# Hymba-style encoder block on one Trainium2 core: a12's quarter of the second half loaded in the raw ring, the x2 loads and pair sums spread over the stages, and the first last block in two passes

## The chip, the cores and the metric

The kernel runs on one core of one Trainium2 chip. The engines are called PE (matrix product), DVE (vector), ACT (scalar), POOL (GpSimd) and SP (which here issues the DMA transfers). The metric is the device time of one execution in microseconds (us); the figure for the kernel before is a median of three timed runs. A trace of one more execution, taken by the hardware profiler, shows each instruction.

## The reference

The block takes x of 2048 tokens by 1024 features and adds three residual terms: a mixer (short convolution and bidirectional gated linear attention), cross-attention into 256 memory rows, and an MLP. A final RMSNorm closes it. The change touches only the end of it:

```python
def sq_relu_mlp(x, mlp_norm, w_up, w_down):
    h = rms_norm(x, mlp_norm) @ w_up          # 1024 -> 4096
    return jnp.square(jax.nn.relu(h)) @ w_down  # 4096 -> 1024
...
        x = x + sq_relu_mlp(x, mlp_norm[l], w_up[l], w_down[l])
    return rms_norm(x, final_norm)
```

All is float32. The kernel keeps that accuracy by splitting each operand into a rounded high part and a low rest, and by forming three products: high by high, high by low, low by high.

## The kernel before, in words

Features lie on the 128 partitions and tokens on the free axis. A tile of a product is 128 features by 512 tokens and fills one PSUM bank; there are eight banks, four named `ps` and four named `pg`, which the code takes in turn. Tiles in SBUF come from rings of fixed depth: `a` (28 tiles of 128x1024, for operands and for the residual x2), `g` (8, for split weights), `st` (2 tiles of 128x2048), `raw` and `cv` (3 each, for what has just been loaded), `t` (7) and `gt` (8). A load into a ring waits until the last reader of that ring's oldest tile is done. SP issues the DMA transfers in one fixed order, so a load that waits for its tile holds up all loads behind it. Three helpers stand behind most rows of the profile: `split` (L117 the high part on ACT, L118 the low part on DVE), `add` (L928, on DVE unless POOL is named) and `mm3` (L145 to L147, three matmuls).

**Up projection.** It is done in two halves of the tokens (`hf` = 0, 1), each with the seven products of a Strassen-like scheme for every one of 16 weight steps f (L1013). `token_side` prepares the seven token operands: it loads four quarters of the normalised tokens (a11, a22, a21, a12) from the DRAM tile `x2d` by `quarter` (loads at L956, scaling in four operations at L960), then adds, subtracts and splits. a11, a21 and a12 lie in the `st` ring, a22 in `raw` and `cv`. As `st` has two tiles, which a11 and a21 hold, a12's loads wait until a11 has been read for the last time. The token side of the second half is made while the last steps of the first half run. `weight_side` loads each step's weights into `raw` and `cv` (L990), and forms and splits the seven weight operands. The results, squared after the ReLU, go out to the DRAM tile `zu` (L1019, L1023).

**Down projection.** 28 of the 32 row tiles of `w_down` are taken in four groups of 4, 4, 3 and 3 pairs (GROUPS). For each group, `half_steps` yields 14 steps: seven products for each of two token halves c, in the order 1, 2, then 5, 3, then 6, 4 and 7, each pair of lines for c = 0 and c = 1. `token_operands` reads `zu` back (L1125 into `raw` and `cv`, L1152 into `st`) and combines the pieces on POOL or DVE; `weight_operands` reads `w_down` (L1171) into `t` and `gt` and subtracts on POOL. Operands are prepared up to three steps ahead. Each step has four banks (d = 0 to 3) of 12 matmuls each (L1243, 9 in the groups of 3). Products 2 and 3 go on in the banks of 1 and 5. Each bank is then evicted by `add` into the residual `acc`, or into `sums`, the sum u that three quarters of the output share. `acc` holds x2, eight d by two c, in 16 tiles of the `a` ring, loaded by `load_acc` (L1218): d 0 to 3 ahead of the loop, d 4 to 7 at step 0. After the loop, 24 additions on DVE (128x512) put the shared sums into three quarters of `acc`: the pair sums, which the trace shows as `a<-a,a`.

**Last blocks.** The remaining four row tiles (REST) are added in five blocks of tokens by `column`: for each d of eight one bank with 12 matmuls over j = 0 to 3, eviction into `acc`, square on ACT, and the sum of the squares on POOL (DVE in the last block). `rest_u` loads and splits the four token operands of a block, `load_w` the four weight operands. `finish` turns the sum of squares of a block into the RMSNorm's factors and scales and stores the block's output (L1287) while the next block's matmuls run. For these blocks the order on PE and DVE is that in which the code is written.

Of the kernel before, what the change touches and what calls it, by code (L numbers as in the profile page):

```python
# [10 lines left out]
F32R = mybir.dt.float32r  # L11
# [6 lines left out]
P = 128  # L18
S = 2048
D = 1024  # L20
KT = D // P
TB = 512
# [8 lines left out]
def block_kernel(ctx, tc, x, mem, wm, wv, wlg, wlog, wout, wxk, wxv, wxqT, wxo, wup, wdn,  # L31
                 vecs, ones, consts, out):
    nc = tc.nc
# [7 lines left out]
    def A4(dt=F32, shape=(P, 1024)):  # L41
        return big.tile(list(shape), dt, tag="a", name="a4", bufs=NA)
# [7 lines left out]
    def RAW(shape=(P, 1024)):  # L50
        return big.tile(list(shape), F32, tag="raw", name="raw", bufs=3)

    def CV():
        return big.tile([P, 1028], F32, tag="cv", name="cv", bufs=3)
# [54 lines left out]
    zu = dram.tile([FF, S], F32, name="zu")  # L109
# [6 lines left out]
    def split(src, hi, lo):  # L116
        mark["act"] = nc.scalar.copy(hi, src)  # L117
        nc.vector.tensor_tensor(out=lo, in0=src, in1=hi.bitcast(F32), op=ALU.subtract)  # L118
# [10 lines left out]
    def load_w(ap, shape=(P, 1024), T=A4):  # L129
        r = RAW(shape)  # L130
        mark["dma"] = nc.sync.dma_start(r, ap)
        hi, lo = T(F32R, shape), T(F32R, shape)
        split(r, hi, lo)
        return hi, lo
# [8 lines left out]
    def mm3(ps, L, R, first, last):  # L143
        (lh, ll), (rh, rl) = L, R
        nc.tensor.matmul(ps, lh, rh, start=first, stop=False)  # L145
        nc.tensor.matmul(ps, lh, rl, start=False, stop=False)  # L146
        mark["pe"] = nc.tensor.matmul(ps, ll, rh, start=False, stop=last)  # L147
# [31 lines left out]
    def fold(tiles, SQ, eng):  # L179

        acc = None
        for t in tiles:
            sq = SQ()
            nc.scalar.activation(sq, t, AF.Square)
            if acc is None:
                acc = sq
            else:
                eng.tensor_tensor(out=acc, in0=acc, in1=sq, op=ALU.add)
        eng.tensor_tensor(out=acc[:, 0], in0=acc[:, 0], in1=acc[:, 1], op=ALU.add)
        return acc[:, 0]  # L190
# [574 lines left out]
    with tc.manual_schedule(engines={EngineType.PE}):  # L765
# [6 lines left out]
        sq = fold([mt[:, 2 * j:2 * j + 2] for mt in mts for j in range(2)], lambda: T2(F32, (P, 2, NMEM)), nc.vector)  # L772
# [118 lines left out]
    for b in range(4):  # L891
        bs = slice(b * TB, (b + 1) * TB)
        yb, nxt = nxt, []
        if b == 3:

            xts, pss = [], []
# [5 lines left out]
            for kt in range(KT):  # L902
                for d in range(KT):
                    ds = slice(d * P, (d + 1) * P)
# [5 lines left out]
        for dp in range(KT // 2):  # L910
            ld = y_load(b + 1, dp)
            xt = load_T(x, b, dp, CV()[:, :D].rearrange("p (j t) -> p j t", j=2))
            for j in range(2):
                d = 2 * dp + j
                ds = slice(d * P, (d + 1) * P)
                ps = PS()
# [10 lines left out]
    def add(out, a, b, op=ALU.add, eng=nc.vector):  # L927
        eng.tensor_tensor(out=out, in0=a, in1=b, op=op)  # L928
# [11 lines left out]
    def S2():  # L940
        t = ST(F32, (P, 2, 1024))
        return [t[:, i] for i in range(2)]

    def R2():
        return [RAW(), CV()[:, :D]]
# [5 lines left out]
    def quarter(hf, b, k, t):  # L951

        b0 = 2 * hf + b
        for i in range(2):
            r = (4 * k + 2 * i) * P
            nc.sync.dma_start(t[i].rearrange("p (j t) -> p j t", j=2),  # L956
                              x2d[r:r + 2 * P, b0 * TB:(b0 + 1) * TB].rearrange("(j p) t -> p j t", p=P))
        for j, v in enumerate(kts(t)):
            kt = 4 * k + j
            nc.vector.scalar_tensor_tensor(out=v, in0=v, scalar=g_mlp[:, kt:kt + 1], in1=rows[:, b],  # L960
                                           op0=ALU.mult, op1=ALU.mult)
        return t

    def token_side(hf):

        a11 = quarter(hf, 0, 0, S2())
        a22 = quarter(hf, 1, 1, R2())
        a21 = quarter(hf, 1, 0, S2())  # L970
        yield None
        yield 1, operand(a11)
        yield 4, operand(a22)
        s = a22
        both(s, a21, a22, ALU.add)
        yield 5, operand(s)
        both(s, s, a11, ALU.subtract)
        yield 6, operand(s)
        both(a21, a11, a21, ALU.subtract)
        a12 = quarter(hf, 0, 1, S2())  # L980
        yield 2, operand(a12)
        yield 7, operand(a21)
        both(a12, a12, s, ALU.subtract)
        yield 3, operand(a12)
# [131 lines left out]
    GROUPS = [(0, 16, 4), (4, 20, 4), (8, 24, 3), (11, 27, 3)]  # L1116
    REST = (14, 30, 15, 31)
# [96 lines left out]
    def load_acc(ds):  # L1214
        for d in ds:
            for c in range(2):
                acc[d][c] = A4()
                nc.sync.dma_start(acc[d][c], x2d[d * P:(d + 1) * P, c * 1024:(c + 1) * 1024])  # L1218

    halves = [slice(0, TB), slice(TB, 2 * TB)]  # L1220
    steps = half_steps()
    ahead = [next(steps)]
    acc = [[None, None] for _ in range(KT)]
    load_acc(range(4))
    sums = [A4(F32, (P, 2, TB)) for _ in range(4)]
    for i in range(14 * len(GROUPS)):
        while len(ahead) < 3:
            ahead.append(next(steps, None))
        first, p, c, w, x = ahead.pop(0)
        if i == 0:  # L1230
            load_acc(range(4, KT))
        n = len(x)

        chained = p in (2, 3)
        if not chained:
            banks = [(PG if d % 2 == 0 else PS)() for d in range(4)]
        for d in range(4):
            ds = slice(d * P, (d + 1) * P)
            ps = banks[d]
            for k in range(n):  # L1240
                wh, wl = w[k][0][:, ds], w[k][1][:, ds]
                for l, r in ((wh, x[k][0]), (wh, x[k][1]), (wl, x[k][0])):
                    nc.tensor.matmul(ps, l, r, start=not chained and k == 0 and l is wh and r is x[k][0],  # L1243
                                     stop=k == n - 1 and l is wl, skip_group_check=chained)
            o11, o21 = (acc[d][c][:, h] for h in halves)
            o12, o22 = (acc[d + 4][c][:, h] for h in halves)
            u = sums[d][:, c]
            if p == 1 and first:
                nc.scalar.copy(u, ps)
                continue  # L1250
            for o in {1: (u,), 2: (o11,), 6: (u,), 5: (o22,), 3: (o12,), 7: (o21, o22), 4: (o21,)}[p]:
                if p == 4:
                    add(o, o, ps, SUB)
                else:
                    add(o, ps, o)


    def rest_u(b):
        got = []
        for i in range(0, 4, 2):  # L1260
            t = (RAW() if i == 0 else CV()[:, :D]).rearrange("p (j t) -> p j t", j=2)
            for j in range(2):
                f = REST[i + j]
                nc.sync.dma_start(t[:, j], zu[f * P:(f + 1) * P, b * TB:(b + 1) * TB])
            hi, lo = (A4(F32R, (P, 2, TB)) for _ in range(2))
            split(t, hi, lo)
            got += [(hi[:, j], lo[:, j]) for j in range(2)]
        return got

    ur = [rest_u(0)]  # L1270
    wr = [load_w(wdn[f], T=G4) for f in REST]
    for d in range(4):
        for c in range(2):
            u = sums[d][:, c]
            for o in (acc[d][c][:, halves[1]], acc[d + 4][c][:, halves[0]], acc[d + 4][c][:, halves[1]]):
                add(o, o, u, eng=nc.vector)

    def final_sums(sq, n, PT):
        m = n // P
# [7 lines left out]
        nc.vector.scalar_tensor_tensor(out=a, in0=a, scalar=g_fin[:, d:d + 1], in1=r, op0=ALU.mult, op1=ALU.mult)  # L1287
        nc.sync.dma_start(out[d * P:(d + 1) * P, c * 1024 + cs.start:c * 1024 + cs.stop], a)

    def column(us, c, cs, squares, between):  # L1290

        qs = []
        n = cs.stop - cs.start
        o = cs.start % TB
        for d in range(KT):
            ds = slice(d * P, (d + 1) * P)
            ps = (PG if d % 2 == 0 else PS)()[:, :n]
            for j in range(4):
                mm3(ps, (wr[j][0][:, ds], wr[j][1][:, ds]), (us[j][0][:, o:o + n], us[j][1][:, o:o + n]), j == 0, j == 3)
            a = acc[d][c][:, cs]  # L1300
            add(a, ps, a)
            qs.append(GT()[:, :n])
            nc.scalar.activation(qs[-1], a, AF.Square)
            if d > 1:
                add(qs[0], qs[0], qs[d - 1], eng=squares)
            if between is not None:
                next(between, None)
        add(qs[0], qs[0], qs[-1], eng=squares)
        return qs[0]
# [12 lines left out]
    blocks = [(0, cs) for cs in halves] + [(1, halves[0]), (1, slice(TB, TB + TH)), (1, slice(TB + TH, 2 * TB))]  # L1322
    todo = None
    with tc.manual_schedule(engines={EngineType.PE, EngineType.DVE}):
        for n, (c, cs) in enumerate(blocks):
            if n + 1 < 4:
                ur.append(rest_u(n + 1))
            sq = column(ur[min(n, 3)], c, cs, nc.vector if n == len(blocks) - 1 else nc.gpsimd, todo)
            for _ in todo or ():
                pass  # L1330
            todo = finish(c, cs, sq)
        for _ in todo:
            pass
# [60 lines left out]
```

## Time and profile before

| | us |
|---|---|
| median of three timed runs | 2694.26 (2693.18 to 2695.48) |
| profiled execution | 2702.45 |
| its span | 2700.7 |
| MLP up projection, about | 1408 to 2034 |
| MLP down projection, about | 2034 to 2584 |
| last blocks, about | 2584 to 2701 |

The mean granted clock of PE in the profiled execution was 0.983. A timeline row gives the start, the duration, the engine, the line, the operation, output and inputs, the shape and a count; in brackets stands the idle time of the engine ahead of it and what ended that wait. `L118 a<-st,a` is thus a split of a tile of the `st` ring. In a row with a count the duration is that of the whole run of instructions. A row of the table by stretches gives each engine's busy time in a stretch of the span. Some matmul records can be missing from a trace.

### The profile page before, as it was taken

What the parts mean: (1) busy time and instruction counts of PE and PEld (TensorE: products, weight loads), DVE (VectorE), ACT (ScalarE), POOL (GpSimd) and SP (SyncE); (2) the same over time, 40 slices, a digit from 0 to 9 for tenths busy, and PEclk for the clock granted to TensorE, in tenths of its full rate; (3) what the DMA queues carried; (4) which work ended last, traced back from release to release, by engine and by line L of the source; (5) the groups of instructions that cost most, each with busy time, mean ns of one, the idle gap of its engine ahead of it and who ended that gap; (6) DMA issues with size and microseconds to landing.
All of it is one profiled execution on the core that took longest, in us unless ns stands there. A gap on an engine that the chain in (4) does not pass through costs nothing.

```text
span 2700.7 us, 34654 instructions
## 1 busy us (share of the span) xinstructions
PE 2592.5 (96%) x13560; PEld 2207.7 (82%) x13560; DVE 1626.4 (60%) x2502; ACT 933.2 (35%) x1432; POOL 259.6 (10%) x178
## 2 busy tenths in 40 slices
PE   7999999989989999999999999899999899999998
PEld 7898888877777787989997888788887788888877
DVE  6512363467766455344467657766556768687975
ACT  5411153434435343232234333433333223222232
POOL 0000000000010000000000000000003224243223
PEclk9999999999999999999999999999999999999999
DMA  7512354224435452111134333343338664555233
GB/s 253 179 61 69 101 185 162 81 88 121 135 104 175 145 183 94 52 43 48 48 115 166 106 113 106 110 159 107 112 121 290 220 197 150 179 168 174 95 106 110
DMA packets 198309, 353.26 MB, mean 131 GB/s; under 512 B 17345, under 2 KB 73793, under 8 KB 198145
## 3 DMA queue, kind: packets, MB, share of 16 engines
q1 hardware_dynamic: 198144, 351.05, 39.9%
q8 instruction: 106, 1.74, 0.3%
q14 instruction: 59, 0.48, 0.1%
HBM read 262.90 MB, written 88.08 MB: 130 GB/s over the span
## 4 chain that ended last, share of the span: by engine, by line
PE 77%; DVE 10%; DMA 6%; ACT 3%; issue 2%; POOL 0%; SPq 0%; DVEq 0%; POOLq 0%; ACTq 0%
PE ps L1013 12%; PE ps L145 9%; PE ps L147 9%; PE ps L146 9%; PE pg L1243 9%; PE ps L1243 9%; PE pg L1013 9%; PE pg L145 3%; PE pg L147 3%; PE pg L146 2%; DVE a L118 2%; DMA gt<-zv 2%; DVE g L118 1%; DVE st L474 1%; DVE g L400 1%
## 5 line engine op out<-in xcount | busy, mean ns | idle before, releaser
L145 PE MATMUL ps<-a,a 128*128 128x512 f32 (+1 forms) x840 | 306.0, 364 | 6.5 <-DVE t L249 5.9
L146 PE MATMUL ps<-a,a 128*128 128x512 f32 (+1 forms) x840 | 306.0, 364 | 0.0
L147 PE MATMUL ps<-a,a 128*128 128x512 f32 (+1 forms) x840 | 305.1, 363 | 0.0
L1243 PE MATMUL pg<-a,g 128*128 128x512 f32 x1176 | 288.6, 392 | 10.1 <-DVE a L928 7.2
L1013 PE MATMUL ps<-a,g 128*128 128x512 f32 x1152 | 284.5, 392 | 7.4 <-ACT a L117 4.4
L1243 PE MATMUL ps<-a,g 128*128 128x512 f32 x1176 | 284.8, 389 | 0.0
L1013 PE MATMUL pg<-a,g 128*128 128x512 f32 x1152 | 279.6, 390 | 1.7 <-ACT g L117 1.1
L1243 PEld LDWEIGHTS pg<-a,g 128*128 128x128 f32 x1176 | 221.7, 189 | 59.1 <-issue 7.6
L1013 PEld LDWEIGHTS ps<-a,g 128*128 128x128 f32 x1152 | 217.4, 189 | 54.1 <-ACT a L117 5.0
L1243 PEld LDWEIGHTS ps<-a,g 128*128 128x128 f32 x1176 | 220.8, 188 | 45.9
L1013 PEld LDWEIGHTS pg<-a,g 128*128 128x128 f32 x1152 | 216.4, 188 | 48.4 <-ACT g L117 2.0
L117 ACT CAST a<-raw 128x1024 fp32r<-128x1024 f32 (+1 forms) x126 | 127.9, 1022 | 346.0 <-PE ps L1243 112.1
L118 DVE TENSOR_TENSOR a<-raw,a 128x1024 fp32r<-128x1024 f32 (+1 forms) x126 | 156.0, 1246 | 117.3 <-ACT a L117 115.9
L117 ACT CAST g<-gt 128x512 fp32r<-128x512 f32 x180 | 103.8, 618 | 349.0 <-PE pg L1013 197.2
L145 PEld LDWEIGHTS ps<-a,a 128*128 128x128 f32 x840 | 161.6, 192 | 32.6 <-DVE t L249 4.7
L146 PEld LDWEIGHTS ps<-a,a 128*128 128x128 f32 x840 | 162.0, 193 | 23.2 <-issue 0.2
L147 PEld LDWEIGHTS ps<-a,a 128*128 128x128 f32 x840 | 161.7, 192 | 23.3 <-issue 0.2
L118 DVE TENSOR_TENSOR g<-gt,g 128x512 fp32r<-128x512 f32 x180 | 133.4, 780 | 44.7 <-ACT g L117 44.7
L928 POOL TENSOR_TENSOR gt<-gt,t 128x512 f32<-128x512 f32 x42 | 79.4, 1908 | 815.9 <-DMA t<-in_wdn 746.9
L928 DVE TENSOR_TENSOR t<-pg,t 128x512 f32<-128x512 f32 x64 | 44.2, 691 | 172.0 <-issue 126.3
L928 DVE TENSOR_TENSOR a<-pg,a 128x512 f32<-128x512 f32 (+1 forms) x128 | 84.1, 668 | 62.3 <-PE pg L1243 46.1
L118 DVE TENSOR_TENSOR g<-raw,g 128x1024 fp32r<-128x1024 f32 (+3 forms) x90 | 98.7, 1107 | 35.6 <-ACT g L117 35.5
(323 smaller groups left out, 5157.7 us busy)
## 6 DMA issues: line engine op xcount, KB each, us to landing
raw<-zu SPq DMA_DIRECT2D x64, 512.0 KB, 4.1
t<-in_wdn SPq DMA_DIRECT2D x84, 256.0 KB, 4.1
raw<-in_wm SPq DMA_DIRECT2D x32, 512.0 KB, 4.1
raw<-in_wup SPq DMA_DIRECT2D x32, 512.0 KB, 4.1
cv<-in_wup SPq DMA_DIRECT2D x32, 512.0 KB, 4.9
zu<-gt SPq DMA_DIRECT2D x64, 256.0 KB, 2.4
zu<-t SPq DMA_DIRECT2D x64, 256.0 KB, 3.9
cv<-zu SPq DMA_DIRECT2D x32, 512.0 KB, 5.0
```

What stands on the lines that cost most here:

```text
L117: mark["act"] = nc.scalar.copy(hi, src)
L118: nc.vector.tensor_tensor(out=lo, in0=src, in1=hi.bitcast(F32), op=ALU.subtract)
L145: nc.tensor.matmul(ps, lh, rh, start=first, stop=False)
L146: nc.tensor.matmul(ps, lh, rl, start=False, stop=False)
L147: mark["pe"] = nc.tensor.matmul(ps, ll, rh, start=False, stop=last)
L400: nc.vector.tensor_tensor_scan(out=Q[hf][:, sl], data0=reset, data1=K[hf][:, sl], initial=0.0, op0=ALU.mult, op1=ALU.add)
L474: nc.vector.scalar_tensor_tensor(out=St[r, a], in0=St[r, b], scalar=de[r, a:a + 1], in1=St[r, a], op0=ALU.mult, op1=ALU.add)
L928: eng.tensor_tensor(out=out, in0=a, in1=b, op=op)
L1013: nc.tensor.matmul(ps, W[w][:, ks], X[x][kt], start=first and kt + w + x == 0, stop=kt == 3 and w == 1, skip_group_check=not first)
L1243: nc.tensor.matmul(ps, l, r, start=not chained and k == 0 and l is wh and r is x[k][0], stop=k == n - 1 and l is wl, skip_group_check=chained)
```

## The change

Five things change; the number of instructions on each engine's data path doesn't.

- In the second half of the up projection, a12's quarter is loaded right behind a21's, into `raw` and `cv`, not later into `st`. The first half stays.
- The x2 loads: d 0 to 3 at step 0 of the down projection, d 4 to 7 at step 2.
- The pair sums move into `column`, ahead of an eviction each: eight in each of the first three blocks.
- The first last block is made in two passes: j = 0 and 1 for all eight d, each in a bank of its own, then j = 2 and 3 and the evictions.
- `rest_u(0)` and the first REST weights are called two steps before the down projection ends, and the table of where a product is added is written as `goes`.

```diff
@@ token_side
         a21 = quarter(hf, 1, 0, S2())
+        if hf == 1:
+            a12 = quarter(hf, 0, 1, R2())
...
-        a12 = quarter(hf, 0, 1, S2())
+        if hf == 0:
+            a12 = quarter(hf, 0, 1, S2())
@@ down projection
-    load_acc(range(4))
...
-        if i == 0:
-            load_acc(range(4, KT))
+        if i in (0, 2):
+            load_acc(range(2 * i, 2 * i + 4))
+        if i == 14 * len(GROUPS) - 2:
+            ur = [rest_u(0)]
+            wr = [load_w(wdn[REST[0]], T=G4)]
...
-    ur = [rest_u(0)]
-    wr = [load_w(wdn[f], T=G4) for f in REST]
-    for d in range(4):
-        for c in range(2):
-            u = sums[d][:, c]
-            for o in (acc[d][c][:, halves[1]], acc[d + 4][c][:, halves[0]], acc[d + 4][c][:, halves[1]]):
-                add(o, o, u, eng=nc.vector)
+    wr += [load_w(wdn[f], T=G4) for f in REST[1:]]
@@ column
-    def column(us, c, cs, squares, between):
+    def column(us, c, cs, squares, between, passes=1):
...
+        pss = []
+
+        def part(d, js):
+            ds = slice(d * P, (d + 1) * P)
+            for j in js:
+                mm3(pss[d], (wr[j][0][:, ds], wr[j][1][:, ds]), (us[j][0][:, o:o + n], us[j][1][:, o:o + n]), j == 0, j == 3)
+
+        for d in range(KT if passes == 2 else 0):
+            pss.append((PG if d % 2 == 0 else PS)()[:, :n])
+            part(d, (0, 1))
         for d in range(KT):
-            ds = slice(d * P, (d + 1) * P)
-            ps = (PG if d % 2 == 0 else PS)()[:, :n]
-            for j in range(4):
-                mm3(ps, (wr[j][0][:, ds], wr[j][1][:, ds]), (us[j][0][:, o:o + n], us[j][1][:, o:o + n]), j == 0, j == 3)
+            if passes == 1:
+                pss.append((PG if d % 2 == 0 else PS)()[:, :n])
+            part(d, (2, 3) if passes == 2 else range(4))
+            ps = pss[d]
             a = acc[d][c][:, cs]
+
+            if (c, cs.start) != (1, TB) and n == TB:
+                if cs.start == TB or d >= 4:
+                    add(a, a, sums[d % 4][:, c])
+                elif d < 4:
+                    dd = d + 4 * c
+                    late = acc[dd][1][:, halves[1]]
+                    add(late, late, sums[d][:, 1])
             add(a, ps, a)
...
-            sq = column(ur[min(n, 3)], c, cs, nc.vector if n == len(blocks) - 1 else nc.gpsimd, todo)
+            sq = column(ur[min(n, 3)], c, cs, nc.vector if n == len(blocks) - 1 else nc.gpsimd, todo,
+                        2 if n == 0 else 1)
```

What moves on the queues stands below. The lines of the kernel after are shifted by a few: L990 is L993, L1019 is L1022, L1023 is L1026, L1125 is L1128, L1171 is L1174, L1218 is L1221.

SP in the last steps of the first half, the kernel before: weight loads of the next steps (`in_wup`) between the stores of results (`zu`).

```order
485 L1023 DMA zu<-t_13838 128x512
486 L990 DMA raw<-in_wup 128x1024
487 L1023 DMA zu<-t_13876 128x512
488 L990 DMA cv<-in_wup 128x1024
489 L1019 DMA zu<-gt 128x512 x2
490 L1023 DMA zu<-t_13990 128x512
491 L990 DMA raw<-in_wup 128x1024
492 L1023 DMA zu<-t_14028 128x512
```

The same place in the kernel after:

```order
485 L1026 DMA zu<-t_13838 128x512
486 L956 DMA raw<-x2d 128x2x512
487 L1026 DMA zu<-t_13876 128x512
488 L956 DMA cv<-x2d 128x2x512
489 L1022 DMA zu<-gt 128x512 x2
490 L1026 DMA zu<-t_13990 128x512
491 L993 DMA raw<-in_wup 128x1024
492 L1026 DMA zu<-t_14028 128x512
```

The loads of one step's weights are now a12's loads from `x2d`, and that step's weights stand where the next step's stood.

SP at the start of the down projection, the kernel before: the x2 loads into `a` tiles, the stores of the last results, and the loads of weights (`in_wdn`) and of `zu`.

```order
583 L1023 DMA zu<-t_16463 128x512
584 L1125 DMA raw<-zu 128x2x512
585 L1023 DMA zu<-t_16501 128x512
586 L1218 DMA a_16695<-x2d 128x1024
587 L1218 DMA a_16697<-x2d 128x1024
588 L1218 DMA a_16699<-x2d 128x1024
589 L1218 DMA a_16701<-x2d 128x1024
590 L1171 DMA t_16663<-in_wdn 128x512
591 L1171 DMA t_16665<-in_wdn 128x512
592 L1171 DMA t_16667<-in_wdn 128x512
593 L1218 DMA a_16703<-x2d 128x1024
```

The kernel after, from the same store on (`zu` from the last steps of the up projection):

```order
584 L1026 DMA zu<-t_16464 128x512
585 L1128 DMA raw<-zu 128x2x512
586 L1026 DMA zu<-t_16502 128x512
587 L1128 DMA cv<-zu 128x2x512
588 L1128 DMA raw<-zu 128x2x512
589 L1128 DMA cv<-zu 128x2x512
590 L1221 DMA a_16744<-x2d 128x1024
591 L1174 DMA t_16664<-in_wdn 128x512
592 L1174 DMA t_16666<-in_wdn 128x512
593 L1174 DMA t_16668<-in_wdn 128x512
594 L1221 DMA a_16746<-x2d 128x1024
595 L1221 DMA a_16748<-x2d 128x1024
```

Three loads of `zu` now stand ahead of the first x2 load, which before stood further down. Not shown: before, the second eight x2 loads stand in one run (rows 606 to 613) ahead of the next `cv<-zu` and `gt<-in_wdn`; after, they stand in two runs of four (rows 618 to 621 and 625 to 628) behind `gt<-in_wdn` and seven loads of `t`.

DVE at the first last block, the kernel before: the end of the run of 24 pair sums, two splits of the next block's tokens, and evictions (`a<-pg,a` and `a<-ps,a`).

```order
2046 L928 TENSOR_TENSOR a_16707<-a_16707,a_16714 128x512
2047 L928 TENSOR_TENSOR a_16771<-a_16771,a_16714 128x512
2048 L928 TENSOR_TENSOR a_16709<-a_16709,a_16714 128x512
2049 L928 TENSOR_TENSOR a_16773<-a_16773,a_16714 128x512
2050 L118 TENSOR_TENSOR a_20901<-raw,a_20900 128x1024
2051 L118 TENSOR_TENSOR a_20908<-cv,a_20907 128x1024
2052 L928 TENSOR_TENSOR a_16695<-pg,a_16695 128x512
2053 L928 TENSOR_TENSOR a_16699<-ps,a_16699 128x512
2054 L928 TENSOR_TENSOR a_16703<-pg,a_16703 128x512
2055 L928 TENSOR_TENSOR a_16707<-ps,a_16707 128x512
2056 L928 TENSOR_TENSOR a_16759<-pg,a_16759 128x512
2057 L928 TENSOR_TENSOR a_16763<-ps,a_16763 128x512
```

The same place in the kernel after:

```order
2027 L118 TENSOR_TENSOR g_20869<-raw,g_20868 128x1024
2028 L118 TENSOR_TENSOR a_20878<-raw,a_20877 128x1024
2029 L118 TENSOR_TENSOR a_20885<-cv,a_20884 128x1024
2030 L928 TENSOR_TENSOR a_16746<-a_16746,a_16696 128x512
2031 L928 TENSOR_TENSOR a_16744<-pg,a_16744 128x512
2032 L928 TENSOR_TENSOR a_16750<-a_16750,a_16697 128x512
2033 L928 TENSOR_TENSOR a_16748<-ps,a_16748 128x512
2034 L928 TENSOR_TENSOR a_16754<-a_16754,a_16698 128x512
2035 L928 TENSOR_TENSOR a_16752<-pg,a_16752 128x512
2036 L928 TENSOR_TENSOR a_16758<-a_16758,a_16699 128x512
2037 L928 TENSOR_TENSOR a_16756<-ps,a_16756 128x512
2038 L928 TENSOR_TENSOR a_16929<-a_16929,a_16696 128x512
```

Each pair sum now stands directly ahead of an eviction, and the evictions of the first block follow the splits without a run of sums in between.

More of the change, by code (lines that the diff above doesn't have):

```diff
@@ L1218, in load_acc, with rest_u @@
                 nc.sync.dma_start(acc[d][c], x2d[d * P:(d + 1) * P, c * 1024:(c + 1) * 1024])
+    def rest_u(b):
+        got = []
+        for i in range(0, 4, 2):
+            t = (RAW() if i == 0 else CV()[:, :D]).rearrange("p (j t) -> p j t", j=2)
+            for j in range(2):
+                f = REST[i + j]
+                nc.sync.dma_start(t[:, j], zu[f * P:(f + 1) * P, b * TB:(b + 1) * TB])
+            hi, lo = (A4(F32R, (P, 2, TB)) for _ in range(2))
+            split(t, hi, lo)
+            got += [(hi[:, j], lo[:, j]) for j in range(2)]
+        return got
     halves = [slice(0, TB), slice(TB, 2 * TB)]
@@ L1244, in block_kernel @@
                                      stop=k == n - 1 and l is wl, skip_group_check=chained)
-            o11, o21 = (acc[d][c][:, h] for h in halves)
-            o12, o22 = (acc[d + 4][c][:, h] for h in halves)
+            out_ = lambda dd, h: acc[dd][c][:, halves[h]]
             u = sums[d][:, c]
@@ L1250, in block_kernel @@
                 continue
-            for o in {1: (u,), 2: (o11,), 6: (u,), 5: (o22,), 3: (o12,), 7: (o21, o22), 4: (o21,)}[p]:
+            goes = {2: ((d, 0),), 5: ((d + 4, 1),), 3: ((d + 4, 0),), 7: ((d, 1), (d + 4, 1)), 4: ((d, 1),)}
+            for o in [u] if p in (1, 6) else [out_(*g) for g in goes[p]]:
                 if p == 4:
@@ L1255, in block_kernel @@
                     add(o, ps, o)
[L1258 to L1268, printed above, removed]
-    ur = [rest_u(0)]
-    wr = [load_w(wdn[f], T=G4) for f in REST]
-    for d in range(4):
-        for c in range(2):
-            u = sums[d][:, c]
-            for o in (acc[d][c][:, halves[1]], acc[d + 4][c][:, halves[0]], acc[d + 4][c][:, halves[1]]):
-                add(o, o, u, eng=nc.vector)
+    wr += [load_w(wdn[f], T=G4) for f in REST[1:]]
     def final_sums(sq, n, PT):
```

## The prediction

> **What bounds the kernel now.** First the page's shares, to see which engine is the limit on the whole.
>
> ```profile
> span 2700.7 us, 34654 instructions
> PE 2592.5 (96%) x13560; PEld 2207.7 (82%) x13560; DVE 1626.4 (60%) x2502; ACT 933.2 (35%) x1432; POOL 259.6 (10%) x178
> ```
>
> PE is busy 96% of the span and the change takes no matmul away, so only PE's idle and slow-clock time can be won. The table by stretches says where that is (columns: stretch, us; busy us and count of PE, PEld, DVE, ACT, POOL; granted clock; DMA share; GB/s).
>
> ```profile
> 1690.00:1780.00 90.00, 82.82 (x348) 66.69 (x347) 72.19 (x94) 41.29 (x58) 0.00 (x0) 0.96 0.40 127
> 1780.00:2025.00 245.00, 245.00 (x1082) 202.20 (x1081) 143.01 (x217) 89.42 (x143) 0.00 (x0) 1.00 0.36 118
> 2025.00:2120.00 95.00, 85.68 (x363) 68.75 (x362) 65.63 (x62) 29.83 (x42) 29.58 (x14) 0.96 0.82 284
> 2120.00:2580.00 460.00, 459.20 (x2027) 379.93 (x2026) 359.41 (x431) 130.10 (x180) 152.22 (x75) 1.00 0.51 164
> 2584.70:2615.30 30.60, 26.01 (x97) 19.65 (x96) 24.02 (x35) 9.25 (x12) 7.44 (x6) 0.89 0.28 69
> 2615.30:2637.10 21.80, 21.80 (x105) 18.31 (x104) 14.32 (x19) 5.37 (x8) 9.21 (x8) 1.00 0.26 94
> 2637.10:2658.90 21.80, 21.80 (x106) 18.33 (x105) 13.26 (x18) 6.00 (x9) 8.99 (x8) 1.00 0.20 75
> ```
>
> The second row is PE without a gap: 245.00 / 1082 = 0.2265 us per matmul. By that price, row one lost 90.0 - 348 x 0.2265 = 11.2 us (place A, the change of half in the up projection), row three 95.0 - 363 x 0.2265 = 12.8 (place B, the start of the down projection), and the first last block 30.6 - 21.8 = 8.8 (place C; a full block takes 21.8 in the two rows below it). Nothing is lost between. The change works at exactly these three places, so at most 32.8 us are there to win.
>
> **Place A: a12's quarter.** Timelines of PE, DVE and SP, and two rows of the DMA table:
>
> ```profile
> 1686.61 0.33 SPq L990 DMA_DIRECT2D raw<-in_wup  x1
> 1724.28 0.33 SPq L990 DMA_DIRECT2D raw<-in_wup  x1
> 1726.88 0.50 PE L1013 MATMUL ps<-a,g 128*128 128x512 f32 x1 [1.19 <-ACT g L117]
> 1728.59 1.22 DVE L118 TENSOR_TENSOR g<-raw,g 128x1024 fp32r<-128x1024 f32 x1
> 1735.12 0.89 SPq L956 DMA_DIRECT2D st<-x2d  x2
> 1742.18 2.74 DVE L960 SCALAR_TENSOR_TENSOR st<-st,vec,rows 128x512 f32<-128x512 f32 x4 [5.29 <-DMA st<-x2d]
> 1744.73 0.51 PE L1013 MATMUL ps<-a,g 128*128 128x512 f32 x1 [4.41 <-ACT a L117]
> 1746.11 5.06 PE L1013 MATMUL ps<-a,g 128*128 128x512 f32 x11 [0.88 <-DVE a L118]
> 1750.97 3.42 PE L1013 MATMUL pg<-a,g 128*128 128x512 f32 x12
> raw<-in_wup SPq DMA_DIRECT2D x32, 512.0 KB, 4.1
> cv<-in_wup SPq DMA_DIRECT2D x32, 512.0 KB, 4.9
> ```
>
> The loads into st leave only at 1735.12, when the ST slot comes free; DVE waits 5.29 us for them and PE 4.41 + 0.88. Behind the wait, 11 matmuls take 5.06 us instead of 2.49 and 12 take 3.42 instead of 2.72: the halved clock costs another 3.3. Together 8.5. The change loads a12 far ahead, so this wait goes with its tail. The price is in the ring it now uses. The weights of the half's first step move to the request of 1686.61, 38 us ahead of use: free. Those of the second move to that of 1724.28; with 4.1 and 4.9 us to landing they are there at 1728.4 and, from the cv load 1.4 later, 1730.6. DVE, busy until 1729.8 by its row of 1728.59, then has about half a microsecond of slack. The four scalings (2.74 in all) move to about 1677 to 1690, where a12 has landed, ahead of the crowded stretch. What can come back is the next wait: the splits of a21, due one bank (2.7 us) after a12's. I leave 1.0 us for weights and a21 together (0 to 4). The wait of 1.19 is of another cause and stays. **Gain 7.5 (4.5 to 8.5).**
>
> **Place B: x2 loads.** The same views, a group of the page, and one stretch of the table:
>
> ```profile
> 2025.46 1.90 SPq L1171 DMA_DIRECT2D t<-in_wdn  x3
> 2037.96 0.50 PE L1243 MATMUL pg<-a,g 128*128 128x512 f32 x1 [0.84 <-ACT g L117]
> 2045.59 6.50 SPq L1218 DMA_DIRECT2D a<-x2d  x8
> 2052.70 0.37 SPq L1125 DMA_DIRECT2D cv<-zu  x1
> 2066.51 6.50 POOL L928 TENSOR_TENSOR gt<-gt,t 128x512 f32<-128x512 f32 x4 [646.65 <-DMA t<-in_wdn]
> 2074.02 7.42 DVE L118 TENSOR_TENSOR g<-gt,g 128x512 fp32r<-128x512 f32 x3
> 2087.07 2.40 POOL L928 TENSOR_TENSOR st<-st,raw 128x1024 f32<-128x1024 f32 x1
> 2087.07 3.48 DVE L928 TENSOR_TENSOR st<-st,raw 128x1024 f32<-128x1024 f32 x1
> 2107.77 1.21 DVE L928 TENSOR_TENSOR st<-st,cv 128x1024 f32<-128x1024 f32 x1
> 2102.80 4.95 PE L1243 MATMUL pg<-a,g 128*128 128x512 f32 x12 [7.19 <-DVE a L928]
> L118 DVE TENSOR_TENSOR g<-gt,g 128x512 fp32r<-128x512 f32 x180 | 133.4, 780 | 44.7 <-ACT g L117 44.7
> 2068.50:2102.60 34.10, 25.81 (x110) 19.93 (x108) 34.10 (x25) 12.63 (x16) 24.32 (x11) 0.96 0.64 221
> ```
>
> The great wait is 7.19 us for an eviction by DVE, plus 4.95 - 2.72 = 2.2 of slow clock. DVE is late for two reasons. Eight x2 loads hold SP's queue for 6.50 us ahead of the zu load at 2052.70, so operands come late and in a heap; and POOL's sums then run beside DVE's: three splits of g take 7.42 us where the mean of 780 ns makes 2.3, a subtraction 3.48 where it takes 1.21 alone. The change puts three zu loads ahead of the x2 loads, so four splits (4.9 us at 1.22) and POOL's first sum run near 2023 to 2036, before the heap, and the second eight x2 loads go behind the weight loads. The eviction is 7.19 late. Taken off DVE ahead of it: the four splits, 4.9, and the excess of the three splits, 7.42 - 2.34 = 5.1, if POOL's four weight sums (6.50) come ahead of them. That is 10.0 against 7.19; but PE, too, comes some 3 us sooner without its small waits ahead of this place, so I expect DVE 0 to 1 late. New cost: the first x2 load now waits for an A slot that a product of the up projection frees, and three weight loads of the row of 2025.46 stand behind it; the first wait of the stage, 0.84 (2037.96), may grow to between 1.7 and 3. Left of the 12.8: about 2.5 there and 1.0 at the eviction. **Gain 9.3**; its ends are 4 (only the four splits' time comes through, less 1 for the start) and 12 (nearly all).
>
> **Place C: two passes and spread sums.**
>
> ```profile
> 2588.93 0.50 PE L146 MATMUL pg<-a,g 128*128 128x512 f32 x1 [1.87 <-DVE a L118]
> 2591.27 0.50 PE L147 MATMUL pg<-a,g 128*128 128x512 f32 x1 [1.83 <-DVE g L118]
> 2591.13 1.28 DVE L928 TENSOR_TENSOR a<-ps,a 128x512 f32<-128x512 f32 x2
> 2592.33 1.22 DVE L118 TENSOR_TENSOR g<-raw,g 128x1024 fp32r<-128x1024 f32 x1
> 2593.46 8.51 DVE L928 TENSOR_TENSOR a<-a,a 128x512 f32<-128x512 f32 x14
> 2629.80 1.29 POOL L928 TENSOR_TENSOR gt<-gt 128x512 f32<-128x512 f32 x1 [2.35 <-ACT gt L1303]
> 2615.53 0.69 DVE L928 TENSOR_TENSOR a<-ps,a 128x512 f32<-128x512 f32 x1 [2.03 <-PE ps L147]
> 2550.93 2.15 DVE L928 TENSOR_TENSOR a<-a,a 128x512 f32<-128x512 f32 x1
> ```
>
> PE wants all four operands within the first bank and waits for each split; the last is done at 2592.33 + 1.22 = 2593.6. With two passes the third and fourth are first wanted after 48 matmuls, 2584.7 + 10.9 = 2595.6: covered. Pass 1's last bank is wanted at 2584.7 + 7 x 1.36 = 2594.2 and cleared at 2592.4 (row of 2591.13). So the 8.8 us go. In exchange pass 2 gives out a bank every 6 matmuls, 1.36 us, and DVE owes for each 0.69 of eviction and 8.51/14 = 0.61 of pair sum: 1.30, with two splits of 1.22 besides. POOL adds 1.29 of squares. Here a rule of the trace weighs: where POOL and DVE's sums of two buffers met (2087.07), DVE took 3.48 while POOL took 2.40; taken in turn a bank costs 0.61 + 1.29 = 1.90. POOL starts when two banks are out and squared, 2595.6 + 2.7 + 1.4 = 2599.7, and seven squares end at 2613.0; PE asks for the total after two banks of the next block, 2606.5 + 5.4 = 2611.9. That is 1.1 late; the two splits put DVE itself 8 x 1.30 + 2.44 - 10.9 = 1.9 behind, the two delays overlap in part, and I take 1.5. Blocks two and three gain 8 x 0.61 = 4.9 us of DVE on 14.32 and 13.26, under 21.8; lag 0.5. **Gain 8.8 - 2.0 = 6.8 (2 to 8.8).** The Trainium skill, page "SBUF — State Buffer", section "Who interferes with whom", says that a VectorE operation with two SBUF operands and GpSimd exclude each other by a lock on a shared port; the pair at 2087.07 agrees. By it C gains 6.8; without any lock POOL would keep pace and C would gain about 8.3.
>
> The other edits are free: which queue rows rest_u(0) and its weights take does not change, and the goes table issues the same additions.
>
> **The sum.** 7.5 + 9.3 + 6.8 = 23.6 us of the profiled 2702.45 gives 2678.85; that run stands 8.2 above the median of 2694.26, which becomes 2670.7, **2671**. A change is told from none here at 0.2%, 5.4 us.
>
> **Rivals.**
> - DVE stays last in B: POOL's sums still meet the splits, only at another time, and the new start wait eats part. For: by the last row shown there DVE was busy in all of the 34.10 us up to the eviction. Against: 4.9 us of splits leave that heap in any case. B gains 3, total 17.3: 2677. Chance 0.17.
> - The ring bites in A: two of the raw buffers hold tokens until about 1743, the second step's weights are late and PE waits twice. For: half a microsecond of slack. Against: 4.1 us is a median with 40% DMA share. A gains 4: 2674. Chance 0.08.
> - Pair sums under POOL become the bound of the last blocks, and the kernel is slower. With x us for one sum, DVE exceeds PE by 2.4 + 8(0.69 + x) - 10.9 in pass 2 and 14.32 + 8x - 21.8 and 13.26 + 8x - 21.8 in the next two: 24x - 19.0. It eats all 7.5 + 9.3 + 8.8 = 25.6 from x = 1.86. At 2.15 (2550.93, the one sum that met POOL) it costs 32.6, net 7 more: 2701. Against: POOL works 9 us of 21.8 there, so not every sum can meet it. Chance 0.05; a mild form that takes all of C's gain leaves 16.8: 2677.5, chance 0.04.
> - Nothing comes of it: each wait gone shows the next engine just behind it. For: three engines stand close in each place. Against: three independent places would all have to fail. 2694, chance 0.05.
>
> A clock rule bears on C too: the Trainium skill, page "TensorE: Matmul & The Clock Gate", section "What's actually happening", says that the clock halves after an idle window of about 3.4 us. The 4.41 and 7.19 agree; in C no wait passed 1.87, yet the granted clock fell to 0.89 over the block. By the rule alone C's tail would not exist; the measured row decides.
>
> **Numbers.** The forecast keeps 0.61. Its ends: all upper gains, 8.5 + 12 + 8.8 = 29.3, and A's small waits of some 2 as well, 2662; all lower ones, 4.5 + 4 + 2 = 10.5, 2684, and 1.1 of spread of the runs, 2685. Only the slower case and the empty one lie outside (0.10), with the tails. Faster 0.61 + 0.17 + 0.08 + 0.04 = 0.90, same 0.05, slower 0.05.
>
> **What would show it.** Right: no wait of PE above 1 us near 1740; no wait of 7 us for a DVE eviction near 2095, and x2 loads in SP's queue in pieces; a first last block of 22 to 24 us with the pair sums between evictions near 0.6 us each. Wrong: PE waiting for weights near 1731; a first wait of the down projection of over 3 us; pair sums of 1 us or more and PE waiting for banks or for the squares' total in blocks two and three; a new stretch at half clock anywhere.

## The result, and the profile after

The changed kernel took 2674.52 us (median of four runs, 2673.82 to 2674.85) against 2693.72 us for the kernel before (four runs): a ratio of 0.9928, with a 95% interval of 0.9912 to 0.9944, or 19 us. On another chip, beside the experiments, it was 2678.91 against 2695.18: 0.9942 (0.9930 to 0.9955). The page of the changed kernel:

```profile
span 2672.0 us, 34688 instructions
PE 2580.3 (97%) x13560; PEld 2199.2 (82%) x13560; DVE 1627.1 (61%) x2502; ACT 934.0 (35%) x1432; POOL 259.9 (10%) x178
```

The two profiled spans differ by 28.7 us, more than the medians. Most of the excess is not the change's: the group of matmuls just ahead of place A starts at 1721.30 before and at 1715.29 after, 6.0 us apart, through code that is the same in both. In the traces of the experiments, whose early code is the same too, this mark lies between 1713.1 and 1721.7. So the places are compared here by durations between two marks within one trace. The marks are four PE rows, with the same number of matmuls between them in both kernels (248, 3450 and 542); of before:

```profile
1721.30 3.03 PE L1013 MATMUL ps<-a,t 128*128 128x512 f32 x12
1788.69 2.90 PE L1013 MATMUL ps<-a,t 128*128 128x512 f32 x12
2584.74 0.39 PE L145 MATMUL pg<-a,g 128*128 128x512 f32 x1
2692.10 1.22 PE L169 MATMUL pg<-cst,sm 128*128 128x128 f32 x4 [1.03 <-POOL sm L153]
```

and of after:

```profile
1715.29 3.02 PE L1016 MATMUL ps<-a,t 128*128 128x512 f32 x12
1774.85 2.89 PE L1016 MATMUL ps<-a,t 128*128 128x512 f32 x12
2561.82 0.39 PE L145 MATMUL pg<-a,g 128*128 128x512 f32 x1
2664.40 0.71 PE L169 MATMUL pg<-cst,sm 128*128 128x128 f32 x4 [1.03 <-POOL sm L153]
```

First to second mark is place A, second to third holds place B, third to fourth is place C up to the last row factors. In this one pair of traces A gave 67.39 - 59.56 = 7.8 us, B 796.05 - 786.97 = 9.1, C 107.36 - 102.58 = 4.8. The stretches of after that answer to those shown of before:

```profile
1684.00:1766.00 82.00, 79.63 (x347) 64.52 (x346) 69.32 (x90) 41.09 (x58) 0.00 (x0) 1.00 0.46 151
2012.00:2100.00 88.00, 85.18 (x372) 68.98 (x371) 57.30 (x62) 27.77 (x40) 27.48 (x15) 1.00 0.88 306
2561.80:2583.60 21.80, 21.80 (x98) 18.04 (x97) 19.74 (x27) 7.64 (x10) 5.60 (x4) 1.00 0.37 97
2583.60:2605.50 21.90, 20.31 (x97) 16.49 (x96) 19.18 (x24) 5.52 (x9) 10.94 (x8) 1.00 0.19 68
2605.50:2628.00 22.50, 22.01 (x104) 17.91 (x103) 19.84 (x27) 6.69 (x10) 10.06 (x7) 1.00 0.20 75
```

The granted clock is 1.00 in all of them, where before it was 0.96, 0.96 and 0.89 at the three places. The first last block is PE without a gap, 21.80 of 21.80. The two rows below it, without loss before, now have some (20.31 of 21.90).

**Place A after** (SP, DVE, PE). The quarter's loads leave at 1659.74; the second step's weights leave at 1718.27, DVE waits 0.82 us there, and PE's waits of 4.41 and 0.88 are down to one of 0.47, with 11 matmuls in 2.79 us behind it:

```profile
1659.74 0.37 SPq L956 DMA_DIRECT2D raw<-x2d  x1
1718.27 0.33 SPq L993 DMA_DIRECT2D raw<-in_wup  x1
1724.60 1.23 DVE L118 TENSOR_TENSOR g<-raw,g 128x1024 fp32r<-128x1024 f32 x1 [0.82 <-ACT g L117]
1732.96 2.79 PE L1016 MATMUL ps<-a,g 128*128 128x512 f32 x11 [0.47 <-DVE a L118]
```

**Place B after.** The zu load stands ahead of the first x2 load. Counted from the second mark, POOL's first sum of `zu` pieces starts at 242.84 us instead of 284.29 (2072.98 before), its weight sums at 269.68 instead of 277.82. The wait of 7.19 us is 1.24, and 0.39 in the second trace of this kernel:

```profile
2009.50 0.37 SPq L1128 DMA_DIRECT2D cv<-zu  x1
2013.95 0.33 SPq L1221 DMA_DIRECT2D a<-x2d  x1
2017.69 2.40 POOL L928 TENSOR_TENSOR st<-st,raw 128x1024 f32<-128x1024 f32 x1 [603.42 <-DMA raw<-zu]
2021.96 0.73 PE L1260 MATMUL pg<-a,g 128*128 128x512 f32 x2 [1.02 <-ACT g L117]
2044.53 6.00 POOL L928 TENSOR_TENSOR gt<-gt,t 128x512 f32<-128x512 f32 x4 [22.11 <-DMA t<-in_wdn]
2072.60 5.72 DVE L118 TENSOR_TENSOR g<-t,g 128x512 fp32r<-128x512 f32 x2
2081.94 2.99 PE L1260 MATMUL pg<-a,g 128*128 128x512 f32 x12 [1.24 <-DVE a L928]
```

DVE still meets POOL (two splits in 5.72 us at 2072.60), but later and less.

**Place C after.** DVE's pair sums (`a<-a,a`), an eviction (`a<-ps,a`) and a split, POOL's additions of squares and its power for the factors (L153), and PE's waits:

```profile
2576.23 0.68 DVE L928 TENSOR_TENSOR a<-a,a 128x512 f32<-128x512 f32 x1
2577.05 3.00 POOL L928 TENSOR_TENSOR gt<-gt 128x512 f32<-128x512 f32 x2 [34.74 <-ACT gt L1320]
2577.59 1.31 DVE L928 TENSOR_TENSOR a<-a,a 128x512 f32<-128x512 f32 x1
2578.82 0.68 DVE L928 TENSOR_TENSOR a<-ps,a 128x512 f32<-128x512 f32 x1
2584.76 1.00 DVE L928 TENSOR_TENSOR a<-a,a 128x512 f32<-128x512 f32 x1
2587.36 1.83 POOL L928 TENSOR_TENSOR gt<-gt 128x512 f32<-128x512 f32 x1 [0.40 <-ACT gt L1320]
2587.97 2.31 DVE L118 TENSOR_TENSOR a<-cv,a 128x1024 fp32r<-128x1024 f32 x1
2592.98 0.15 DVE L151 TENSOR_SCALAR sm<-ps 128x4 f32<-128x4 f32 x1
2593.21 1.39 POOL L153 TENSOR_TENSOR sm<-sm,nhalf 128x4 f32<-128x4 f32 x1 [4.02 <-DVE sm L151]
2594.66 1.16 PE L169 MATMUL pg<-cst,sm 128*128 128x128 f32 x8 [1.53 <-POOL sm L153]
2600.54 1.47 DVE L928 TENSOR_TENSOR a<-a,a 128x512 f32<-128x512 f32 x1
2615.39 1.05 PE L1281 MATMUL ps<-vec,gt 128*128 128x1 f32 x8 [0.49 <-POOL gt L928]
2637.99 1.05 PE L1281 MATMUL ps<-vec,gt 128*128 128x1 f32 x8 [1.04 <-POOL gt L928]
```

A pair sum takes 0.68 us until POOL begins at 2577.05. Of all 24 sums, 13 run while one of POOL's additions does and take 0.93 to 1.77 us; the other 11 take 0.68. An eviction reads one of its two inputs from PSUM, and it stays at 0.68 to 0.69 beside the same additions. The two splits of the first block take 1.57 and 2.31 instead of 1.22. The small step that turns the total into factors (L151) stands behind them in DVE's order, so PE waits 1.53 for the factors in the second block and 0.49 and 1.04 for the totals of the next two: 3.06 us in all.

### The profile page after: what moved, and what is told of

It reads as the page before. It is cut to its first block, busy times and chain, and to the rows that moved or that the text cites. A ratio compares the mean times of both kernels' runs of the same rounds, so it can differ in the third digit from the quotient of the medians.

```text
span 2672.0 us, 34688 instructions
## 1 busy us (share of the span) xinstructions
PE 2580.3 (97%) x13560; PEld 2199.2 (82%) x13560; DVE 1627.1 (61%) x2502; ACT 934.0 (35%) x1432; POOL 259.9 (10%) x178
## 4 chain that ended last, share of the span: by engine, by line
PE 79%; DVE 10%; DMA 5%; ACT 3%; issue 2%; POOL 1%; SPq 0%; DVEq 0%; POOLq 0%; ACTq 0%
PE ps L1016 12%; PE pg L1260 10%; PE ps L1260 10%; PE ps L145 9%; PE ps L147 9%; PE ps L146 9%; PE pg L1016 9%; PE pg L145 2%; PE pg L146 2%; PE pg L147 2%; DVE a L118 2%; DMA gt<-zv 1%; DVE st L474 1%; DMA raw<-zy 1%; DVE a L928 1%
## 5 line engine op out<-in xcount | busy, mean ns | idle before, releaser
L153 POOL TENSOR_TENSOR sm<-sm,nhalf 128x2 f32<-128x2 f32 (+1 forms) x26 | 24.3, 933 | 991.2 <-DVE sm L151 991.2
L117 ACT CAST g<-raw 128x1024 fp32r<-128x1024 f32 (+3 forms) x90 | 85.4, 959 | 97.6 <-PE ps L146 17.7
```

The lines of the kernel that those rows point to most:

```text
L153: nc.gpsimd.tensor_tensor(out=r, in0=v, in1=nhalf[:, :n], op=ALU.pow)
```

## The experiments

The timed intervals are 0.2 to 0.6% wide, so the stretches between marks carry the reading. All in us:

| kernel | ratio (95%) | A | B | C |
|---|---|---|---|---|
| before | 1 | 67.39 | 796.05 | 107.36 |
| after | 0.9928 (0.9912 to 0.9944) | 59.56 | 786.97 | 102.58 |
| after, again | 0.9942 (0.9930 to 0.9955) | 60.35 | 785.77 | 104.10 |
| a12 alone | 0.9966 (0.9955 to 0.9978) | 60.39 | 795.31 | 105.49 |
| x2 loads alone | 0.9964 (0.9952 to 0.9976) | 65.96 | 786.32 | 106.15 |
| a12 and x2 | 0.9951 (0.9938 to 0.9964) | 60.38 | 786.24 | 106.83 |
| two passes alone | 1.0002 (0.9993 to 1.0011) | 67.25 | 796.93 | 107.47 |
| spread sums alone | 1.0011 (1.0003 to 1.0020) | 66.70 | 795.55 | 108.37 |
| after, late factors | 0.9927 (0.9913 to 0.9941) | 60.35 | 786.77 | 98.44 |
| the same, early sums | 0.9920 (0.9907 to 0.9934) | 60.40 | 784.78 | 98.04 |
| after, no squares on POOL | 0.9897 (0.9868 to 0.9926) | 60.46 | 786.86 | 98.11 |
| after, no pair sums | 0.9906 (0.9877 to 0.9935) | 59.62 | 786.18 | 98.41 |
| all x2 loads at step 0 | 0.9975 (0.9962 to 0.9987) | 66.70 | 791.32 | 105.95 |
| last eight x2 loads late | 0.9953 (0.9930 to 0.9976) | 66.51 | 785.66 | 106.68 |

**The a12 edit alone:**

```diff
+        if hf == 1:
+            a12 = quarter(hf, 0, 1, R2())
...
+        if hf == 0:
+            a12 = quarter(hf, 0, 1, S2())
```

> The kernel before with the first edit alone (a12 of the second half in raw and cv). Theory of independent places: in the trace of the full change place A gave 7.8 us, measured between the products of the third operand ahead of it and behind it; alone it gives the same, 7 to 8.5 us, ratio 0.9970. Rival, the place gains only while later stages catch it up: the down projection waits for the same x2 and zu loads, so what is gained at the change of half is waited for again at the start of the down projection, and under 3 us is left, ratio 0.999 to 1.000.

Measured: A 60.39, 6.4 us under the mean of the traces without the edit, a little less than expected; B and C within the scatter of the others. The gain stays where it is made; the rival, that the down projection waits for it again, falls. The great wait of place B is still there, 7.21 for 7.19:

```profile
2091.39 5.07 PE L1246 MATMUL pg<-a,g 128*128 128x512 f32 x12 [7.21 <-DVE a L928]
```

**The x2 loads alone:**

```diff
-    load_acc(range(4))
...
-        if i == 0:
-            load_acc(range(4, KT))
+        if i in (0, 2):
+            load_acc(range(2 * i, 2 * i + 4))
```

> The kernel before with the x2 loads alone moved to steps 0 and 2. Theory: place B gave 9.0 us in the trace of the full change and gives 8 to 10 alone, ratio 0.9966, with the wait of 7.2 us for a DVE eviction down to 1 or 2. Rival, the weights behind the x2 loads decide: half of it, 4 to 5 us, ratio 0.998, and the great wait stays above 3 us.

Measured: B 786.32, and the wait for the eviction 1.18:

```profile
2090.34 1.83 PE L1242 MATMUL pg<-a,g 128*128 128x512 f32 x7 [1.18 <-DVE a L928]
```

The theory holds; which part of the edit does it is asked below.

**Two passes alone, the burst of pair sums kept** (of `column`, only `part`, `pss` and `passes`).

> The kernel before with two passes in the first last block, the burst of pair sums kept ahead of it. Theory: the waits for the four splits (8.8 us with their tail) go whole, and what comes back is the total of the squares, late behind the burst of 14 pair sums, by about 3.5 us once; net 5 us, ratio 0.998, about what the full change got at place C (4.8). Rival, without the spread the burst takes the place of the splits: PE waits for banks or for the total for 6 us and more, net under 2 us, ratio above 0.999.

Measured: no gain, 1.0002. The splits make no long wait any more; the burst does. DVE gets to the first eviction only behind 14 pair sums, POOL begins its squares at 2605.62, and PE waits 4.93 us for their total; in the 7 us behind it the granted clock is 0.53:

```profile
2592.89 8.52 DVE L928 TENSOR_TENSOR a<-a,a 128x512 f32<-128x512 f32 x14
2605.62 11.37 POOL L928 TENSOR_TENSOR gt<-gt 128x512 f32<-128x512 f32 x7 [41.49 <-ACT gt L1314]
2617.04 1.53 PE L1282 MATMUL ps<-vec,gt 128*128 128x1 f32 x8 [4.93 <-POOL gt L928]
```

The rival was right: without the spread, the wait moves from the operands to the total.

**Spread sums alone, one pass** (of `column`, only the block with `add(a, a, sums...)`; the burst removed).

> The kernel before with the pair sums spread over three blocks, one pass. Theory: the splits still make PE wait in the first bank, so nothing is won there, and the spread sums make the normalising factors late in three blocks as in the full change (1.8, 0.8 and 1.4 us); slower by 2 to 4 us, ratio 1.001. Rival, the burst was what held the splits back: faster by 3 us or more, ratio 0.999.

Measured: slower by 0.11% (0.03 to 0.20). Both costs stand in one trace, the wait for a split in the first bank and the late total in a later block:

```profile
2580.15 0.50 PE L147 MATMUL pg<-a,g 128*128 128x512 f32 x1 [2.85 <-DVE g L118]
2655.79 1.05 PE L1277 MATMUL ps<-vec,gt 128*128 128x1 f32 x8 [1.06 <-POOL gt L928]
```

So the two edits to the last blocks are worth nothing or less one by one; only together do they gain. The earlier call of `rest_u(0)` has no run of its own, and that it is free is not shown by one; its first load leaves 21.56 us ahead of the third mark in the kernel before and 21.72 in the full change, so it hardly moved in the queue.

**a12 and x2 together, the last blocks as before:**

> The kernel before with a12's quarter and the x2 loads changed, the last blocks as before. Theory of independent places: 7.4 + 9.3 = 17 us, ratio 0.9938, and the full change lies 3 to 5 us below this kernel. Rival, the last blocks give nothing in the full change (two passes alone gave 0, the spread alone cost 3): this kernel stands level with the full change, ratio 0.9928.

Measured: A 60.38 and B 786.24, as alone: by the stretches the places add up, 16.1 us together and 6.4 + 9.6 alone. The medians are too coarse for that: 13.1 us of the expected 17, against 9.6 and 8.6 alone. C is 106.83. By the medians of one chip this kernel lies 3 us above the full change (2682.04 and 2678.91), with intervals that overlap; by the traces C differs by 106.83 - 104.10 = 2.7.

**The full change once more:**

> The full change once more, beside its parts on one chip: 19 to 21 us under the kernel before, ratio 0.9926; in its trace the same four waits in the last blocks as before (1.53, 0.49, 1.04 and none above 2).

Measured: 16 us, less than expected. The waits are the same (1.48, 0.50, 1.07), but C takes 1.5 us more than in the first trace, for a reason told at the end.

**The total and the factors asked for one bank later:**

```diff
     def finish(c, cs, sq):
+        wide = cs.stop - cs.start == TB
         yield
+        if wide:
+            yield
         rc = final_sums(sq, cs.stop - cs.start, PS)
         yield
+        if wide:
+            yield
         r = to_rows(rc, PG)
```

> The full change with the total of the squares and the row factors each asked for one bank later in the next block. Theory: what the full change gives back in the last blocks is PE waiting in order for the total and the factors (1.53, 0.49 and 1.04 us seen); asked for later, they are ready, and 3 us are won, ratio 0.9915 against the kernel before. Rival, DVE is behind by its own load and the wait only moves to the banks: within 1 us of the full change, 0.9928.

Measured: C 98.44. The first three blocks are PE without a gap, though DVE's work is the same and its busy time in them is no less (19.99 against 19.74 in the first):

```profile
2568.80:2590.60 21.80, 21.80 (x98) 18.04 (x97) 19.99 (x27) 7.64 (x10) 5.62 (x4) 1.00 0.36 97
2590.60:2612.40 21.80, 21.80 (x106) 18.33 (x105) 19.48 (x24) 6.16 (x10) 12.69 (x9) 1.00 0.13 47
2612.40:2634.20 21.80, 21.80 (x106) 18.33 (x105) 19.72 (x26) 6.95 (x10) 9.67 (x8) 1.00 0.20 75
```

By the stretch this is 4 to 5.7 us better than the full change; the timed runs on that chip show 2 us (2676.74 and 2678.91), and their intervals overlap. The ratio of 0.9927 alone would fit the rival as well; the trace decides, as no wait moved to the banks.

**The same, and 16 pair sums early**, four after each of four of the last steps of the down projection; the eight of the second block stay:

```diff
+        k = i - 14 * len(GROUPS) + 5
+        if 0 <= k < 4:
+            for o, c_ in ((acc[k][1][:, halves[1]], 1), (acc[k + 4][0][:, halves[0]], 0),
+                          (acc[k + 4][1][:, halves[1]], 1), (acc[k + 4][1][:, halves[0]], 1)):
+                add(o, o, sums[k][:, c_])
```

> As the run with late factors, and 16 of the 24 pair sums made in the last steps of the down projection, the shared sum being complete, so that the first and the third block carry none. Theory: DVE has some 13 us of idle time there against 10 of sums; the first block's end no longer lags, 0 to 1.5 us more than late factors alone, ratio 0.991. Rival, the sums there meet POOL's subtractions and delay splits or evictions, PE waits in the last steps of the down projection: 2 to 4 us slower than late factors alone, ratio 0.9925.

Measured: 2672.79, the fastest of that chip, 6 us under the full change by the medians. The last 60 us of the down projection stay without a gap with 51.41 us of DVE in them:

```profile
2503.60:2563.50 59.90, 59.90 (x266) 49.61 (x265) 51.41 (x67) 18.04 (x24) 10.33 (x5) 1.00 0.38 118
```

By the stretches 0.4 is added to the late factors in C, and 2.0 in B, where the other traces with the x2 edit scatter by 1.2; so by the stretches most of what beats the full change is the late asking. By the medians it is the smaller part, 2.2 of 6.1 us; which share is whose is not shown.

**Is the lag DVE's own load, or its meeting POOL?** Two runs with work left out, so that their output is not the block's.

> The full change without POOL's additions of squares in the first four blocks (the normalising factors there come from the first feature tile alone). From the start of the last blocks to the last row factors the full change took 102.6 and 104.1 us, the kernels with the old last blocks 105.5 to 107.4, the late factors 98.4. Theory: POOL beside DVE stretches the pair sums (0.99 to 1.48 us instead of 0.61) and the splits (1.57 and 2.31 instead of 1.22), and that lag is what PE waits for; without POOL they are short again, PE's waits of 1.53 and 0.49 us go, and the stretch takes 98 to 99.5 us. Rival, DVE's own load of one pair sum a bank and two splits is the lag: the waits stay, 101 us or more.

Measured: C 98.11, no wait of 0.49 or more ahead of the tail. Without POOL's additions the pair sums and splits are short all through, here near the end of the first block:

```profile
2585.43 0.68 DVE L928 TENSOR_TENSOR a<-a,a 128x512 f32<-128x512 f32 x1
2586.82 1.22 DVE L118 TENSOR_TENSOR a<-raw,a 128x1024 fp32r<-128x1024 f32 x1
2587.96 1.22 DVE L118 TENSOR_TENSOR a<-cv,a 128x1024 fp32r<-128x1024 f32 x1
```

> The full change with the 24 pair sums left out (three quarters of the output lack the shared sum). Theory: without pair sums DVE has 5 us of room in each block although POOL still adds squares, the factors come in time as in the kernel before, and the stretch of the last blocks takes 98 to 99 us, the same as without POOL's additions: both are needed for the lag. Rival, POOL alone makes the total late (seven additions in a row of 1.3 us after two passes): 100 us or more, with a wait for POOL's squares.

Measured: C 98.41. Either one taken away ends the lag. In both runs the step to the factors (L151) behind the first block starts 28.18 us behind the third mark, in the full change 31.16. (The total of that block came in time in all three, so this comparison does not hang on the missing squares.) POOL's additions do not come late by themselves, and DVE's sums don't either; the lag is their meeting. The splits still meet POOL in the run without sums (1.97 and 2.31), and PE does not wait for it. This is what the Trainium skill, page "SBUF — State Buffer", section "Who interferes with whom", calls an exclusive lock, and these two runs agree: 0.68 without POOL, up to 1.77 with it.

**Which part of the x2 edit works?** First all 16 loads at step 0:

```diff
-    load_acc(range(4))
...
-            load_acc(range(4, KT))
+            load_acc(range(KT))
```

> The kernel before with all 16 x2 loads at step 0: the three zu loads go ahead of them, but the last eight are no longer held back behind the weight loads. From the end of the change of half to the start of the last blocks the kernel before took 795.3 to 796.1 us, the kernels with the x2 edit 785.8 to 787.0. Theory of the prediction: the edit works in two parts, the four splits and POOL's first sums early (zu ahead, 4.9 us off DVE) and POOL's weight sums early (last eight behind the weights, 5.1 us): this half gives 4 to 6 us, 790 to 792. Rival, the early zu alone suffices: 787 to 788.

Then the first eight where they were and the last eight at step 2:

```diff
-        if i == 0:
+        if i == 2:
             load_acc(range(4, KT))
```

> The kernel before with its first eight x2 loads where they were, ahead of zu, and the last eight at step 2, behind the weight loads. Theory of the prediction: this is the other half, POOL's weight sums and the zu load no longer wait for eight x2 loads, 3 to 5 us, 791 to 793, and PE still waits 2 to 4 us for a DVE eviction near the first product 5. Rival, holding back the last eight alone suffices, as it takes the 6.5 us out of SP's queue: 787 to 788.

Measured: B 791.32 and 785.66. With all loads at step 0, twelve of them stand in SP's queue for 10.27 us, POOL's weight sums start 279.41 us behind the second mark (277.82 before), and a wait of 3.32 for the eviction is left:

```profile
2035.56 10.27 SPq L1218 DMA_DIRECT2D a<-x2d  x12
2088.68 3.75 PE L1242 MATMUL pg<-a,g 128*128 128x512 f32 x8 [3.32 <-DVE a L928]
```

With the last eight held back, POOL's weight sums start 267.66 us behind the second mark, and the next `zu` load leaves 258.06 behind it instead of 264.01, so that two splits come out of the heap as well (1.23 and 1.22 us at 2047.98, where the kernel before had 2.32 and 1.72). PE has no wait at the eviction at all; its only one in the stage is the first:

```profile
2032.25 0.50 PE L1243 MATMUL pg<-a,g 128*128 128x512 f32 x1 [0.97 <-ACT g L117]
2050.12 5.12 POOL L928 TENSOR_TENSOR gt<-gt,t 128x512 f32<-128x512 f32 x4 [635.67 <-DMA t<-in_wdn]
```

So the theory is right for the first run (790 to 792) and wrong for the second (791 to 793): the rival, that holding back the last eight suffices, gave even more than it said. Holding back the last eight is the whole gain of B; `zu` ahead of x2 gives half of it alone and nothing on top that these traces show.

## Why the prediction was right, and where not

Means over the traces of the table: A 66.75 us in six traces without the edit, 60.19 in eight with it; B 795.96 in four and 786.44 in seven (without the early sums, which also shorten it); C 106.41 in six and 103.34 in two. That makes 6.6 + 9.5 + 3.1 = 19.2; the medians differ by 19.2 in the first measurement and 16.3 in the second. Forecast were 7.5, 9.3 and 6.8.

- **That the places are independent and add up**: shown for A and B by the kernels with one edit or two, whose other stretches stay as they were.
- **Place A**: right in mechanism and size (6.6 to 7.8 for 7.5). The tight slack at the second step's weights was real, a wait of 0.82 for DVE, and PE did not feel it.
- **Place B**: the sum was right, the working was not. The step "that is 10.0 against 7.19" added the four early splits (4.9) and the shortened splits (5.1) as two parts that are both needed. Either one relieves DVE, and they overlap: all x2 loads at step 0 gave 4.6 (795.96 - 791.32), the last eight held back gave 10.3, both together 9.5. The first wait of the stage was forecast at 1.7 to 3; it is 1.02 + 0.33 + 0.23 = 1.6, and 0.9 in the other trace. Neither changed the sum by much, but that 9.3 came so close to 9.5 is in part luck.
- **Place C, the first block**: right. Pass 1 covers the splits, and the block takes 21.80.
- **Place C, what is given back**: the term that was mis-sized. The forecast was 2.0 us, 1.5 for a late total in the first block and 0.5 of lag in two blocks. Measured against 98.2, where neither sums nor squares disturb, it is 102.58 - 98.2 = 4.4, and 5.9 in the second trace. By the means 106.4 - 98.2 = 8.2 us were there to win, where the forecast had 8.8, and 5.1 of them were given back. The steps that failed: "Blocks two and three gain 8 x 0.61 = 4.9 us of DVE ... lag 0.5" took the price of a lone pair sum into blocks where POOL adds squares for about half of the time; over the three blocks, the 13 sums that met it took 8.2 us more than at 0.68 each; and the order of DVE was left out, in which the factors' step stands behind pair sums and splits. The total of the first block, which the forecast called late, came in time; the factors behind it did not. The 1.90 us that the forecast took for a bank with both was near what came (1.70 to 1.89 us from eviction to eviction).
- **The rival of the pair sums under POOL** was thus the mechanism at work, at a fraction of its price. At x = 1.86 for every sum it would have eaten everything; 13 of the 24 sums met POOL, at 0.93 to 1.77.
- **"Nothing comes of it"** describes one thing well, two passes alone: the next wait stood right behind the one removed.

C of the old form scatters between 105.49 and 107.36 from trace to trace, and all of it lies in the first block: behind it PE has no wait before the tail in any of the six traces. The waits in that block add up to 3.9 to 4.5 us. The granted clock over its first 32 us is 0.89 in five of the traces and 0.95 in the one with 105.49. Why the clock recovers sooner in that one stays open.

## What to carry to other kernels

Before a burst is spread, look at which engine shares its blocks: a sum priced alone (0.61 us) took up to 1.77 beside another engine's additions. When a wait for operands is hidden, ask at once what stands next in the waiting engine's order; here two edits that were worth nothing alone were worth 3 us together, and two more `yield`s, asking for a result one bank later, 4 us by the trace (2 us by the timed runs, not clear of their scatter). And price overlapping reliefs of one engine by the larger, not by their sum: here 4.6 and 10.3 us alone made 9.5 together.

## What was not expected of the hardware

One stretch around the total of the third block shows two executions of the same kernel; in the first the wait was 1.04 us, in the second 1.07:

```profile
2636.00:2643.00 7.00, 5.96 (x50) 5.75 (x50) 2.14 (x6) 1.63 (x4) 4.31 (x5) 1.00 0.00 1
```

```profile
2641.00:2648.00 7.00, 5.93 (x38) 5.73 (x37) 1.01 (x3) 1.42 (x4) 4.10 (x5) 0.76 0.00 0
```

In the second the granted clock fell to 0.76 over 7 us, and from this total to that of the next block it took 14.95 us instead of 13.46. The spread sums alone, another kernel, had a wait of 1.06 at the same place, a clock of 0.78 over 7 us and 14.96 us to the next total. So a single wait of about 1 us can cost 1.5 us more in one execution and nothing in the next. The Trainium skill, page "TensorE: Matmul & The Clock Gate", section "What's actually happening", has the clock halve after an idle window of about 3.4 us; here it fell after less, and the measurement decides. The four traces without these waits (late factors, early sums, no squares, no pair sums) have C between 98.04 and 98.44.
